# Output projection by seven products of sums: the last product accumulates in PSUM, the last stage runs in program order, weight sums are stored later, two small reorderings

## The chip, the cores and the metric

The kernel runs on 1 core of one Trainium2 chip (trn2). The metric is the device time of one execution in microseconds, from the first to the last work of the core. Three executions are given for the kernel before; one further execution was profiled.

## What is computed

One layer of a hybrid backbone, D_MODEL 1024, 1024 latent tokens and 256 context tokens. Cut to what matters here:

```python
mod = jax.nn.silu(c) @ w_ada + b_ada
shift, scale, gate = jnp.split(mod, 3, axis=-1)
hl = rmsnorm(x, norm_g) * (1.0 + scale) + shift
zl = jnp.split(hl @ w_in, PROJ_SPLITS, axis=-1)
ya = short_conv_branch(zl[0], zl[1], zl[2], zl[3], conv_sc)
yb = neighbourhood_attention(heads(zl[4]), heads(zl[5]), heads(zl[6]), kc, vc, rpb) * jax.nn.silu(zl[7])
yc = conformer_branch(zl[8], zl[9], zl[10], conv_cf, conv_cf_b, ln_cf_g, ln_cf_b)
y = jnp.concatenate([ya, yb, yc], axis=-1) @ w_out
x = x + gate * y
return rmsnorm(x, final_g)
```

All inputs are fp32. `kc` and `vc` come from the context tokens through the same weights. The conformer branch has a depthwise convolution of 31 taps and a layer norm.

## The kernel before, in words

**Precision.** Every matmul operand is split into two fp32r parts (`split`, L127): ScalarE copies the high part, VectorE or GpSimd subtracts it to get the low part. A product is three matmuls: high by high, high by low, low by high.

**Stages.** (1) `start` (L978): loads, the adaLN matmuls and the normalised, transposed input, in an order written out by hand in the string `SEQ` (L51). A letter is an operation, a digit its block: `B` are the adaLN matmuls of a block, `R` the copy of their result by ScalarE, `C` its four transposes and the shift and scale made of them by VectorE, `f` and `u` the modulation (ScalarE) and the split (VectorE) of a block of the input, `m` the six matmuls that use it, `D` matmuls on zeros that keep TensorE active. (2) The input projections, with four head pairs of attention between them. In each step of `attention` (L531) a block of scores (L596, L597) goes to PSUM, VectorE adds the bias and takes the minimum (L601), ScalarE takes the exponential (L604), GpSimd normalises (L606), TensorE transposes (L615), the result is split (L619, L620) and multiplied by the values (L627). Keys are split into `kt` by `sink_k` (L368). Weights of the projections are loaded into `wr` by SP (L310) and split into `wh` and `wl` by ScalarE and GpSimd (L129, L130). (3) The output projection, at the end of `build`.

**Background work.** `spawn` and `poll` (L95, L105) interleave generators with the matmuls: a generator yields the microseconds of planned matmul time after which its next piece is issued. Two of them are touched here. `out_weights` (L852) makes four sums of quarters of `w_out` in eight blocks (GpSimd subtracts, the result is split, SP stores it to DRAM as `T1` to `T4`, L874). `cf_norm` (L703) transposes the convolution's result in two groups for each half, normalises it on VectorE with a reciprocal root from GpSimd (L271), and transposes it back (L734).

**Order of the engines.** TensorE runs in program order. On VectorE (DVE), ScalarE (ACT), GpSimd (POOL) and SP a scheduler sets the order, except in `start`.

**The output projection.** `y` (1024 by 1024) and `w_out` are taken as 2 by 2 quarters A and B and multiplied by seven products of sums (Winograd's form of Strassen's scheme) instead of eight. One product of a half by a half is 48 matmuls of 512 columns: four row tiles by four blocks of the inner dimension by three parts. The products in order: A11 B11 and A12 B21 (their sum is C11, rows 0 to 3 in half `h0`), S2 T2 (added to A11 B11, called `u` or U2), S1 T1 (with U2 it makes `v`, which belongs to C12 and C22), S3 T3, S4 B22 (to C12: rows 0 to 3, half `h1`), A22 T4 (to C21: rows 4 to 7, half `h0`). C22 is rows 4 to 7, half `h1`. `out_mm4` (L915) issues a product with the inner blocks outside and the four row tiles inside, so all four finish within its last twelve matmuls.

**After the products.** `out_part` (L927): VectorE multiplies a result in PSUM by the gate (L933), adds it to the residual `xres` (L934), and ScalarE sums the squares (L941). `out_gain` (L943) multiplies by `final_g` on GpSimd (L945), `out_mean` (L947) turns the first sum of squares into a mean (L951). When both halves of a row tile are there, `out_scale` (L956) makes the reciprocal root on GpSimd (L961, L964), ScalarE scales the half that has its gain (L967), VectorE scales the other one (L971), and SP stores both (L975). Of row tile 7 the last product comes in two halves of 256 columns.

GpSimd's eight instructions on `u` (four tiles by two), L1263 to L1270:

```python
for t in range(4):
    V.tensor_tensor(out=u[t], in0=ps[t], in1=u[t], op=ALU.add)
    self.out_part(t + 4, h1, 0, ps[t], lp, S)
    self.out_mean(t + 4, 0)
    G.tensor_tensor(out=u[t], in0=u[t], in1=self.gate[:, h0], op=ALU.mult)
    x = self.xres[t + 4][0][:, h0]
    G.tensor_tensor(out=x, in0=x, in1=u[t], op=ALU.add)
    self.out_gain(t + 4, h1)
```

## Time and profile before

| | |
|---|---|
| median of 3 executions | 626.82 us (626.68 to 627.6) |
| the profiled execution | 627.2 us, of which the span of the instructions is 625.2 us |
| TensorE (PE) busy | 582.7 us, 93% of the span, 3041 matmuls |
| VectorE (DVE) busy | 439.3 us, 70% |
| ScalarE (ACT) busy | 264.6 us, 42% |
| GpSimd (POOL) busy | 241.8 us, 39% |
| chain that ended last, by engine | PE 58%, DVE 12%, SP's queue 9%, DMA 6%, POOL 6%, ACT 4%, issue 4% |
| DMA | 98.56 MB, mean 158 GB/s |

How to read it: a busy share is an average over all stages, and matmuls overlap, so a duration of one is longer than the distance to the next. The chain that ended last is followed back from the last instruction to whatever released it. "Idle before" is the time an engine stood still ahead of an instruction, with what ended it. The granted clock (PEclk) is a share of TensorE's full clock: 1.00 is 2.4 GHz, 0.50 is 1.2 GHz. Times in the rows are microseconds from the start of the span.

### The profile page before, as it was taken

The page shows a single profiled execution, that of the slowest core. Times are in us where ns is not written, and L with a number is a line of the kernel's source. Part 1 is how long each engine was busy: PE and PEld are TensorE (multiplying, and loading weights), DVE is VectorE, ACT ScalarE, POOL GpSimd, SP SyncE. Part 2 cuts the span into 40 slices and gives each one's busy share as a digit, 9 for nine tenths or more (in the row PEclk, how much of TensorE's full clock was granted, in tenths as well). Part 3 has the DMA queues.
Part 4 walks back from the last instruction along what each step waited for, and adds up shares of the span by engine and source line. Part 5 has one row for each costly group of instructions (what it writes and reads, how often), then busy time and mean ns, then how long its engine had stood idle before and what let it go on. Part 6 is the DMA issues. An engine that isn't in the chain of part 4 may idle for free.

```text
span 625.2 us, 9212 instructions
## 1 busy us (share of the span) xinstructions
PE 582.7 (93%) x3041; PEld 485.7 (78%) x3041; DVE 439.3 (70%) x744; ACT 264.6 (42%) x528; POOL 241.8 (39%) x270
## 2 busy tenths in 40 slices
PE   7799999999997999999999999999999999999950
PEld 5466888888896988798877898888887888788840
DVE  4466989666774699478897666936889446879935
ACT  2455721111444542556523656435554342443223
POOL 1031232001546334555444455345433440055863
PEclk9999999999998999899999999999999999999995
DMA  8991595966435348435257362483310663992224
GB/s 283 357 326 47 186 285 151 117 156 181 125 90 162 87 128 224 111 93 130 70 160 185 78 183 79 120 241 91 98 26 18 216 222 120 383 369 69 69 93 175
DMA packets 114434, 98.56 MB, mean 158 GB/s; under 512 B 27771, under 2 KB 94421, under 8 KB 114389
## 3 DMA queue, kind: packets, MB, share of 16 engines
q1 hardware_dynamic: 112517, 91.44, 50.6%
q10 hardware_dynamic: 1872, 6.55, 2.8%
q8 instruction: 24, 0.39, 0.3%
q14 instruction: 21, 0.17, 0.1%
HBM read 67.46 MB, written 22.68 MB: 144 GB/s over the span
## 4 chain that ended last, share of the span: by engine, by line
PE 58%; DVE 12%; SPq 9%; DMA 6%; POOL 6%; ACT 4%; issue 4%; DVEq 0%; ACTq 0%; POOLq 0%
PE ps_z L329 9%; PE ps_z L331 9%; PE ps_z L330 9%; SPq L509 4%; PE ps_t L615 3%; PE po L627 3%; DMA wr<-in_w_in 3%; DVE acc L692 3%; PE ps_z L419 3%; PE ps_z L421 3%; PE ps_z L420 3%; PE ps_s L596 3%; PE ps_s L597 2%; SPq L364 2%; DMA yc<-gd 1%
## 5 line engine op out<-in xcount | busy, mean ns | idle before, releaser
L329 PE MATMUL ps_z<-h,wh 128*128 128x512 f32 x384 | 152.3, 397 | 0.0
L331 PE MATMUL ps_z<-h,wl 128*128 128x512 f32 x384 | 151.2, 394 | 0.0
L330 PE MATMUL ps_z<-h,wh 128*128 128x512 f32 x384 | 150.7, 393 | 0.0
L130 POOL TENSOR_TENSOR wl<-wr,wh 128x512 fp32r<-128x512 f32 x44 | 60.1, 1370 | 142.8 <-ACT wh L129 136.2
L606 POOL TENSOR_SCALAR pr<-pr,sm 128x640 f32<-128x640 f32 (+1 forms) x64 | 55.7, 871 | 99.8 <-DVE sm L605 88.4
L331 PEld LDWEIGHTS ps_z<-h,wl 128*128 128x128 f32 x384 | 72.6, 189 | 16.3
L692 DVE SCALAR_TENSOR_TENSOR acc<-t,half_w,acc 128x1024 f32<-128x1024 f32 x60 | 82.2, 1369 | 1.2
L330 PEld LDWEIGHTS ps_z<-h,wh 128*128 128x128 f32 x384 | 73.0, 190 | 12.7
L329 PEld LDWEIGHTS ps_z<-h,wh 128*128 128x128 f32 x384 | 73.0, 190 | 12.3
L619 ACT ACTIVATE pw<-ps_t 128x640 fp32r<-128x640 f32 (+1 forms) x64 | 43.4, 679 | 74.2 <-PE ps_t L615 74.1
L601 DVE CUSTOM_DVE_ANT_0 ps_s<-ps_s,bt 128x640 f32<-128x640 f32 (+1 forms) x64 | 50.9, 796 | 26.3 <-PE ps_s L597 24.4
L620 DVE TENSOR_TENSOR pw<-ps_t,pw 128x640 fp32r<-128x640 f32 (+1 forms) x64 | 50.4, 788 | 22.2 <-ACT pw L619 21.8
L604 ACT ACTIVATE pr<-ps_s,mn 128x640 f32<-128x640 f32 (+1 forms) x64 | 49.0, 766 | 18.8 <-DVE mn L601 17.9
L627 PE MATMUL po<-pw,vt 128*128 128x256 f32 x304 | 51.9, 299 | 0.2 <-DVE pw L620 0.2
L129 ACT ACTIVATE wh<-wr 128x512 fp32r<-128x512 f32 x46 | 28.9, 629 | 54.3 <-DMA wr<-in_w_in 34.8
L596 PE MATMUL ps_s<-kt,qd 128*128 128x384 f32 (+1 forms) x128 | 40.5, 338 | 4.9 <-ACT pr L604 4.8
L615 PE MATMUL ps_t<-ident,pr 128*128 128x128 f32 x304 | 43.7, 273 | 0.8 <-DVE sm L605 0.6
L627 PEld LDWEIGHTS po<-pw,vt 128*128 128x128 f32 x304 | 40.5, 190 | 1.0 <-DVE pw L620 0.9
L597 PE MATMUL ps_s<-kt,qd 128*128 128x256 f32 x128 | 35.7, 284 | 3.0 <-DVE kt L380 3.0
L615 PEld LDWEIGHTS ps_t<-ident,pr 128*128 128x128 f32 x304 | 35.3, 141 | 3.2 <-issue 2.2
L130 POOL TENSOR_TENSOR bgp<-bg,bgp 128x256 fp32r<-128x256 f32 x32 | 28.0, 874 | 19.2 <-ACT bgp L129 19.2
L596 PEld LDWEIGHTS ps_s<-kt,qd 128*128 128x128 f32 x128 | 24.1, 188 | 11.9 <-ACT pr L604 9.9
(192 smaller groups left out, 1084.9 us busy)
## 6 DMA issues: line engine op xcount, KB each, us to landing
wr<-in_w_in SPq DMA_DIRECT2D x52, 256.0 KB
wa<-in_w_ada SPq DMA_DIRECT2D x16, 512.0 KB
qd<-qn SPq DMA_DIRECT2D x32, 256.0 KB
wT<-bgp SPq DMA_DIRECT2D x32, 256.0 KB
wt<-wT SPq DMA_DIRECT2D x16, 512.0 KB
vd<-t SPq DMA_DIRECT2D x20, 256.0 KB
x_in<-in_x SPq DMA_DIRECT2D x8, 512.0 KB
t<-in_w_ada SPq DMA_DIRECT2D x16, 256.0 KB
```

Source lines behind the costliest of these rows:

```text
L130: i2 = (eng or nc.vector).tensor_tensor(out=lo, in0=src, in1=f32(hi), op=ALU.subtract)
L329: nc.tensor.matmul(ps, lhsT=wh, rhs=hh, start=(k == 0), stop=False)
L330: nc.tensor.matmul(ps, lhsT=wh, rhs=hl, start=False, stop=False)
L331: self.last = nc.tensor.matmul(ps, lhsT=wl, rhs=hh, start=False, stop=(k == KT - 1))
L596: nc.tensor.matmul(win, lhsT=q[:, b % 4], rhs=kwin, start=(i == 0), stop=(i == 1))
L601: nc.vector.tensor_tensor_reduce(s, s, tb, op0=ALU.add, op1=ALU.min, scale=1.0, scalar=3e38, accum_out=mn)
L604: nc.scalar.activation(out=pr, in_=s, func=AF.Exp, scale=-1.0, bias=mn, accum_out=sm)
L606: nc.gpsimd.tensor_scalar(out=pr, in0=pr, scalar1=sm, scalar2=0.5, op0=ALU.mult, op1=ALU.mult)
L615: nc.tensor.transpose(out=pt[:, c * P:(c + 1) * P], in_=pr[:, c * P:(c + 1) * P], identity=self.ident)
L620: nc.vector.tensor_tensor(out=pw[:, :, 1, :], in0=pv, in1=f32(pw[:, :, 0, :]), op=ALU.subtract)
L627: self.nc.tensor.matmul(po, lhsT=vt[:, vi, h], rhs=pw[:, c], start=(c == 0), stop=(c == n - 1))
L692: self.after_pe(nc.vector.scalar_tensor_tensor(out=acc, in0=u[:, t:t + T], scalar=self.half_w[:, 2 * t + ct:2 * t + ct + 1], in1=acc, op0= ...
```

## The change

Five things are changed. In the output projection the last product, A22 T4, is accumulated in PSUM onto S3 T3, so that their sum is read once; T4 is stored with its sign turned, and U2 times the gate is added to the residual by GpSimd right after S2 T2. The tiles of the last two products are issued with the row tiles outside, and each row tile's scaling stands behind the next tile's addition. From S2 T2 on DVE, ACT, POOL and SP run in program order; the gate's row broadcast (`gate_rows`) moves behind A12 B21, the loads of `xres` 4 to 7 ahead of the split of S3. The weight sums are stored two steps after they are split, with longer gaps between blocks and a step of 2.9 instead of 3.2. `SEQ` has two matmuls on zeros ahead of `C1` and `m1` behind it. `cf_norm` waits 5.5 instead of 3.0 ahead of the transposes back, and 2.0 instead of 3.0 between its groups.

```diff
@@ -52,7 +52,7 @@
 X0 X1 X2 X3 L00 K L01 W00 W10 L10 L11 X4 X5 X6 X7 W01 W11 L20 L21 L30 L31 X8 X9
 q00 q11 r02 q20 x0 x1 q31 r22 x2 x3 D29 B00 D02 B01 a0 w001 R0 a1 w101 C0 a22 D07
 f0 f1 a3 u0 u1 m0 B10
-B11 R1 m1 C1 D03 q40 f2 f3 q51 u2 u3 m2 D03 r42 q60 q70 x4 x5 r62 x60 x7 m3 D02
+B11 R1 D02 C1 q40 f2 f3 m1 q51 u2 u3 m2 D02 r42 q60 q70 x4 x5 r62 x60 x7 m3 D02
 b0 b1 g0 v0 g1 v1 w01 w11 B20 n0 b2 B21 n1 R2 b3 g2 v2 g3 v3 n2 C2 a4 n3 f4 u4 a5 f5 u5
 b4 B30 m4 g4 v4 b5 B31 g5 v5 R3 m5 C3 n4 a6 f6 u6 a7 f7 u7 q80 n5 b6 g6 v6 q90 m6 b7 g7 v7 r82 m7 x8 n6 x9
 O Q00 c0 c1 h0 o0 h1 o1 Q01 n7 c2 c3 h2 o2 h3 o3 Q02 Q10 Q11 Q12
@@ -726,7 +726,7 @@
                                             op0=ALU.subtract, op1=ALU.mult)
                 vts.append(vt)
                 self.pe(0.43)
-                yield 3.0
+                yield (2.0, 5.5)[g]
             for ct in range(2):
                 ps = self.ps_z.tile([P, HALF], F32, name="ps_z", tag="z")
                 for j in range(4):
@@ -853,6 +853,11 @@
 
         nc = self.nc
         n = 256
+        kept = []
+
+        def put(name, p, i, c):
+            nc.sync.dma_start(out=self.wtd[name][:, :, i, c:c + n], in_=f32(p))
+
         for i in range(4):
             for c in range(0, HALF, n):
                 def raw(k, half):
@@ -862,16 +867,19 @@
 
                 b11, b12, b21, b22 = raw(i, 0), raw(i, 1), raw(4 + i, 0), raw(4 + i, 1)
                 t1 = pool.tile([P, n], F32, name="bg", bufs=5)
-                yield gap
-                for name, out, x, y in (("T1", t1, b12, b11), ("T3", b12, b22, b12), ("T2", t1, b22, t1), ("T4", t1, t1, b21)):
+                yield 2 * gap
+                for name, out, x, y in (("T1", t1, b12, b11), ("T3", b12, b22, b12), ("T2", t1, b22, t1), ("T4", t1, b21, t1)):
                     self.after_pe(nc.gpsimd.tensor_tensor(out=out, in0=x, in1=y, op=ALU.subtract))
                     yield gap
+                    if kept:
+                        put(*kept.pop())
                     p = pool.tile([P, 2, n], F32R, name="bgp", bufs=2)
-                    i1, i2 = self.split(p[:, 0], p[:, 1], out, nc.gpsimd)
-                    self.after_pe(i1)
-                    self.after_pe(i2)
+                    for ins in self.split(p[:, 0], p[:, 1], out, nc.gpsimd):
+                        self.after_pe(ins)
+                    kept.append((name, p, i, c))
                     yield gap
-                    nc.sync.dma_start(out=self.wtd[name][:, :, i, c:c + n], in_=f32(p))
+                yield gap
+        put(*kept.pop())
 
     def load_wt(self, name, pool):
         w = [pool.tile([P, 2, HALF], F32R, name="wt", bufs=8) for _ in range(4)]
@@ -930,7 +938,11 @@
         xt, ss = self.xres[tt]
         n = cs.stop - cs.start
         g = lp.tile([P, HALF], F32, name="fg", bufs=2)[:, 0:n]
-        nc.vector.tensor_tensor(out=g, in0=ps[:, 0:n], in1=self.gate[:, cs], op=ALU.mult)
+        ps = ps if isinstance(ps, list) else [ps[:, 0:n]]
+        m = n // len(ps)
+        for i, p in enumerate(ps):
+            c = cs.start + i * m
+            nc.vector.tensor_tensor(out=g[:, i * m:(i + 1) * m], in0=p, in1=self.gate[:, c:c + m], op=ALU.mult)
         nc.vector.tensor_tensor(out=xt[:, cs], in0=xt[:, cs], in1=g, op=op)
         if eng is nc.vector:
 
@@ -1150,7 +1162,7 @@
         stv.close()
         self.qp = r(self.pool("qp", 2, side="right"))
         self.pp = r(self.pool("pp", 2, side="right"))
-        self.spawn(self.out_weights(r(self.pool("bg", 1, side="right")), 3.2), 4.0)
+        self.spawn(self.out_weights(r(self.pool("bg", 1, side="right")), 2.9), 4.0)
         self.q_first = self.q_parts(0, 0)
         fill = itertools.chain(self.cf_in(1), *(f(ct) for ct in range(2) for f in (self.sc_in, self.sc_mid, self.sc_out)))
         self.run(self.proj_gate(0))
@@ -1214,7 +1226,6 @@
                 S.activation(out=u[t], in_=ps[t], func=AF.Copy)
             for tt in range(4):
                 self.out_tile(tt, lp)
-            self.gate_rows(ps_g)
 
             s1 = []
             for i in range(4):
@@ -1228,6 +1239,7 @@
             t2 = self.load_wt("T2", wt)
             s2 = self.y_parts(yc, [y[i][:, h0] for i in range(4)])
             self.out_mm4(ps, a12, b21, False, skip=True)
+            self.gate_rows(ps_g)
             t1 = self.load_wt("T1", wt)
             s1 = self.y_parts(yc, s1)
             raw = [self.load_b(yc, 1, 1, q, name="yc") for q in (0, 2)]
@@ -1235,58 +1247,67 @@
                 self.out_part(t, h0, 0, ps[t], lp, S)
                 self.out_mean(t, 0)
                 self.out_gain(t, h0)
+            E = mybir.EngineType
+            es.enter_context(tc.manual_schedule(engines={E.DVE, E.Activation, E.Pool, E.SP}))
             ps = banks(g=True)
             self.out_mm4(ps, s2, t2)
             t3 = self.load_wt("T3", wt)
-            s3 = self.y_parts(yc, [y[i][:, h1] for i in range(4)])
+            for tt in range(4, 8):
+                self.out_tile(tt, lp)
             for t in range(4):
                 V.tensor_tensor(out=u[t], in0=ps[t], in1=u[t], op=ALU.add)
-            for tt in range(4, 8):
-                self.out_tile(tt, lp)
+                v = lp.tile([P, HALF], F32, name="fw", bufs=2)
+                x = self.xres[t + 4][0][:, h0]
+                G.tensor_tensor(out=v, in0=u[t], in1=self.gate[:, h0], op=ALU.mult)
+                G.tensor_tensor(out=x, in0=x, in1=v, op=ALU.add)
+            s3 = self.y_parts(yc, [y[i][:, h1] for i in range(4)])
             ps = banks()
             self.out_mm4(ps, s1, t1)
+            s4 = self.y_parts(yc, [y[4 + i][:, h0] for i in range(4)])
             b22 = self.load_wt("B22", wt)
             for q in (0, 2):
                 self.split_b(b22, raw[q // 2], q)
-            s4 = self.y_parts(yc, [y[4 + i][:, h0] for i in range(4)])
             for t in range(4):
-                v = lp.tile([P, HALF], F32, name="fv", bufs=2)
-                V.tensor_tensor(out=v, in0=ps[t], in1=u[t], op=ALU.add)
+                v = u[t]
+                V.tensor_tensor(out=v, in0=ps[t], in1=v, op=ALU.add)
                 V.tensor_tensor(out=v, in0=v, in1=self.gate[:, h1], op=ALU.mult)
                 for tt, eng in ((t + 4, V), (t, G)):
                     x = self.xres[tt][0][:, h1]
                     eng.tensor_tensor(out=x, in0=x, in1=v, op=ALU.add)
-            ps = banks(g=True)
-            self.out_mm4(ps, s3, t3)
+
+            q = [slice(c, c + 256) for c in (0, 256)]
+            ps7 = banks(g=True)
+            ps7q = [ps7[3][:, 0:256], banks(1)[0][:, 0:256]]
+            for i in range(4):
+                for t in range(3):
+                    self.out_mm(ps7[t], i, t, s3, t3, i == 0, i == 3, skip=True)
+                for j in range(2):
+                    self.out_mm(ps7q[j], i, 3, s3, t3, i == 0, i == 3, q[j].start, q[j].stop, skip=True)
             t4 = self.load_wt("T4", wt)
             a22 = self.y_parts(yc, [y[4 + i][:, h1] for i in range(4)])
             for t in range(4):
-                V.tensor_tensor(out=u[t], in0=ps[t], in1=u[t], op=ALU.add)
-                self.out_part(t + 4, h1, 0, ps[t], lp, S)
+                self.out_part(t + 4, h1, 0, ps7[t] if t < 3 else ps7q, lp, S)
                 self.out_mean(t + 4, 0)
-                G.tensor_tensor(out=u[t], in0=u[t], in1=self.gate[:, h0], op=ALU.mult)
-                x = self.xres[t + 4][0][:, h0]
-                G.tensor_tensor(out=x, in0=x, in1=u[t], op=ALU.add)
                 self.out_gain(t + 4, h1)
-            ps = banks()
-            self.out_mm4(ps, s4, b22)
-            for t in range(4):
-                self.out_part(t, h1, 1, ps[t], lp, S)
-                self.out_scale(t, 1, ((h0, S, sync), (h1, None, sync)))
-            ps = banks(3, True)
-            for t in range(3):
+            ps = banks(3)
+            ps = ps + ps[0:1] + ps7
+            for t in range(7):
                 for i in range(4):
-                    self.out_mm(ps[t], i, t, a22, t4, i == 0, i == 3)
-                self.out_part(t + 4, h0, 1, ps[t], lp, S, ALU.subtract)
-                self.out_scale(t + 4, 1, ((h1, S, sync), (h0, None, sync)))
-
-            ps = banks(2)
-            q = [slice(c, c + 256) for c in (0, 256)]
+                    if t < 4:
+                        self.out_mm(ps[t], i, t, s4, b22, i == 0, i == 3)
+                    else:
+                        self.out_mm(ps[t], i, t - 4, a22, t4, False, i == 3, skip=True)
+                cs = h1 if t < 4 else h0
+                self.out_part(t, cs, 1, ps[t], lp, S)
+                if t:
+                    self.out_scale(t - 1, 1, last)
+                last = (h0 if t < 4 else h1, S, sync), (cs, None, sync)
             for j in range(2):
                 for i in range(4):
-                    self.out_mm(ps[j], i, 3, a22, t4, i == 0, i == 3, 256 * j, 256 * j + 256)
-                self.out_part(7, q[j], 1 + j, ps[j], lp, (S, V)[j], ALU.subtract)
+                    self.out_mm(ps7q[j], i, 3, a22, t4, False, i == 3, q[j].start, q[j].stop, skip=True)
+                self.out_part(7, q[j], 1 + j, ps7q[j], lp, (S, V)[j])
                 if j == 0:
+                    self.out_scale(6, 1, last)
                     self.out_gain(7, q[0])
                     self.out_mean(7, 1)
             self.out_scale(7, 2, ((h1, S, act), (q[0], V, None), (q[1], None, sync)))
```

**TensorE, in the first stage, after the adaLN matmuls of block 1 (L220).** `ps_a` is that block's PSUM tile, `ada_row` its copy, `ps_z` with `h` are the matmuls of an input block. Before:

```order
L220 MATMUL ps_a<-wa,stat 32x512 x8
L1066 MATMUL ps_z<-h_82,wh 128x512
...
L1069 MATMUL ps_z<-h_83,wh 128x512 x2
L232 MATMUL ps_a<-ident,ada_row 128x128 x4
L1036 MATMUL ps_z<-zero,ones_r 128x512 x3
```

Now:

```order
L220 MATMUL ps_a<-wa,stat 32x512 x8
L1048 MATMUL ps_z<-zero,ones_r 128x512 x2
L232 MATMUL ps_a<-ident,ada_row 128x128 x4
L1078 MATMUL ps_z<-h_82,wh 128x512
...
L1081 MATMUL ps_z<-h_83,wh 128x512 x2
```

The four transposes of `ada_row` stand ahead of the six matmuls of `m1`, behind two matmuls on zeros.

**SP's queue, at the start of head pair 1.** `qd` are queries, `wr` weights of the gate's projection, `wT` stores of weight sums, `bg` loads for them. Before:

```order
L364 DMA qd<-qn 64x2x512 x2
L874 DMA wT_69<-bgp 256x1x256
L364 DMA qd<-qn 64x2x512
L874 DMA wT_71<-bgp 256x1x256
L364 DMA qd<-qn 64x2x512
L860 DMA bg<-in_w_out 128x256 x3
L310 DMA wr<-in_w_in 128x4x128 x2
L874 DMA wT_70<-bgp 256x1x256
```

Now:

```order
L364 DMA qd<-qn 64x2x512 x4
L310 DMA wr<-in_w_in 128x4x128 x2
L859 DMA wT_69<-bgp 256x1x256
L865 DMA bg<-in_w_out 128x256
L310 DMA wr<-in_w_in 128x4x128 x2
```

Two stores and three loads for the weight sums no longer stand ahead of the first two weight loads.

**GpSimd, in the output projection.** `fu` (and `fw`) is U2 or v, `wt` the split of B22, `fv` the v of before. Before:

```order
L130 TENSOR_TENSOR wt<-yc,wt 128x512 x3
L1258 TENSOR_TENSOR xres<-xres,fv 128x512
L130 TENSOR_TENSOR wt<-yc,wt 128x512
L1258 TENSOR_TENSOR xres<-xres,fv 128x512 x3
L1267 TENSOR_TENSOR fu_5591<-fu_5591,gate 128x512
L1269 TENSOR_TENSOR xres<-xres,fu_5591 128x512
...
L1267 TENSOR_TENSOR fu_5597<-fu_5597,gate 128x512
L1269 TENSOR_TENSOR xres<-xres,fu_5597 128x512
...
L945 TENSOR_TENSOR xres<-xres,fgam 128x512
L961 TENSOR_SCALAR fss<-fss 128x1
```

Now:

```order
L1261 TENSOR_TENSOR fw<-fu_5589,gate 128x512
L1262 TENSOR_TENSOR xres<-xres,fw 128x512
...
L1261 TENSOR_TENSOR fw<-fu_5595,gate 128x512
L1262 TENSOR_TENSOR xres<-xres,fw 128x512
L130 TENSOR_TENSOR wt<-yc,wt 128x512 x4
L1276 TENSOR_TENSOR xres<-xres,fu_5589 128x512
...
L957 TENSOR_TENSOR xres<-xres,fgam 128x512
L973 TENSOR_SCALAR fss<-fss 128x1
```

The eight instructions on U2 stand ahead of the split of B22 and of v, and no longer among the gains ahead of the first reciprocal root.

## Rows read from the trace of the kernel before

**Rows 1.** Busy time by stretch: length, then PE, PEld, DVE, ACT, POOL, PEclk, DMA.

```profile
580.00:591.00 11.00, 11.00 (x49) 9.03 (x49) 10.95 (x17) 2.90 (x8) 8.85 (x8) 1.00 0.22 73
591.00:602.30 11.30, 11.28 (x61) 9.55 (x60) 2.48 (x3) 1.45 (x4) 10.57 (x12) 1.00 0.00 0
602.30:625.20 22.90, 0.00 (x0) 0.00 (x0) 13.83 (x24) 9.90 (x20) 7.73 (x16) 0.60 0.49 183
```

**Rows 2.** The chain that ended last, from 600 us on: start, us, what.

```profile
601.61 0.27 POOL fss L961
...
603.77 0.75 DVE xres L971
604.52 0.61 DVE xres L934
...
606.98 0.75 DVE xres L971
...
620.41 0.35 DVE xres L969
```

**Rows 3.** GpSimd's busy time from its first gain to the first reciprocal root.

```profile
549.60:601.60 52.00, 37.53 (x32) 1.00 0.38 134
```

**Rows 4.** Groups by line: shapes, count, busy us, mean ns of one, idle before.

```profile
L1269 POOL TENSOR_TENSOR xres<-xres,fu 128x512 f32<-128x512 f32 x4 | 6.3, 1568 | 0.3
L1267 POOL TENSOR_TENSOR fu<-fu,gate 128x512 f32<-128x512 f32 x4 | 6.2, 1546 | 1.8 <-DVE fu L1264 1.8
L1258 DVE TENSOR_TENSOR xres<-xres,fv 128x512 f32<-128x512 f32 x4 | 6.0, 1498 | 0.0
L130 POOL TENSOR_TENSOR wt<-yc,wt 128x512 fp32r<-128x512 f32 x4 | 5.6, 1409 | 6.8 <-ACT wt L129 5.3 <-issue 1.4
L1258 POOL TENSOR_TENSOR xres<-xres,fv 128x512 f32<-128x512 f32 x4 | 5.6, 1394 | 4.3 <-DVE fv L1255 4.3
```

**Rows 5.** VectorE in order of time.

```profile
556.23 2.07 DVE L1243 TENSOR_TENSOR fu<-ps_g,fu 128x512 f32<-128x512 f32 x3 [1.39 <-PE ps_g L913]
...
567.22 0.69 DVE L1254 TENSOR_TENSOR fv<-ps_f,fu 128x512 f32<-128x512 f32 x1
...
581.26 0.68 DVE L1264 TENSOR_TENSOR fu<-ps_g,fu 128x512 f32<-128x512 f32 x1
...
589.19 1.38 DVE L933 TENSOR_TENSOR fg<-ps_f,gate 128x512 f32<-128x512 f32 x2
...
602.54 0.78 DVE L971 SCALAR_TENSOR_TENSOR xres<-xres,fss,fgam 128x512 f32<-128x512 f32 x1 [9.07 <-POOL fss L964]
```

**Rows 6.** What TensorE waited for: us in total, times, longest.

```profile
PE ps_s L596 <- ACT pr L604: 4.8, 5, 3.0
PE ps_s L597 <- DVE kt L380: 3.0, 2, 1.9
...
PE ps_z L734 <- DVE t L724: 1.6, 2, 1.1
...
PE ps_g L843 <- DMA yc<-gd: 0.5, 1, 0.5
```

**Rows 7.** Busy time by stretch behind 252 us, columns as in Rows 1.

```profile
252.00:254.00 2.00, 2.00 (x7) 1.61 (x7) 1.15 (x3) 0.78 (x2) 1.88 (x2) 0.50 0.36 89
254.00:256.00 2.00, 2.00 (x9) 1.64 (x8) 0.16 (x1) 0.00 (x0) 0.69 (x1) 0.72 0.74 204
```

**Rows 8.** SP's queue and ScalarE in order of time, start of head pair 1.

```profile
246.13 0.98 SPq L310 DMA_DIRECT2D wr<-in_w_in  x2
...
249.98 0.63 ACT L129 ACTIVATE wh<-wr 128x512 fp32r<-128x512 f32 x1 [1.97 <-DMA wr<-in_w_in]
```

**Rows 9.** ScalarE and TensorE in order of time, first stage.

```profile
26.52 0.60 ACT L225 ACTIVATE ada_row<-ps_a 128x512 f32<-128x512 f32 x1 [3.42 <-PE ps_a L220]
...
27.87 0.60 PE L232 MATMUL ps_a<-ident,ada_row 128*128 128x128 f32 x4
...
30.70 0.50 PE L1066 MATMUL ps_z<-h,wh 128*128 128x512 f32 x1 [1.54 <-DVE h L300]
```

## The prediction

> **What bounds the kernel now.** I read the stretches first. TensorE is busy until 602.3 us, all but without a gap in the output projection, and then 22.9 us pass in which it does nothing [rows 1]: the kernel has a TensorE-bound body and a tail. The chain that ended last says who owns the tail. It runs over GpSimd's reciprocal roots, VectorE's scaling and addition and ScalarE's squares, one row tile after the other: from the scaling at 603.77 to the next at 606.98 it is 3.21 us for one tile, and its first piece is the reciprocal root at 601.61 [rows 2]. What the reader is to see next is why that root came so late. VectorE had stood still for 9.07 us for it, from 593.5 on, with PSUM results waiting [rows 5]. GpSimd was not short of time: from 549.6 to 601.6 it was busy 37.5 of 52.0 us [rows 3], 14.5 us idle. But eight of its instructions (U2 times the gate, added to the residual) could start only behind VectorE's addition of S3 T3 to u at 581.26 [rows 5], and they take 6.2 + 6.3 = 12.5 us [rows 4]. So the root waits for work that could not begin earlier, not for too much work. In the body I read TensorE's waits [rows 6] and the clock behind them [rows 7].
>
> My sum is made against the profiled execution: 627.2 us with a span of 625.2, so 2.0 us lie around the span. The median is 0.4 us below that execution. About 0.2% (1.3 us) is what a measurement here can tell from no change.
>
> **The end, part by part.** *GpSimd.* The eight instructions move behind S2 T2, whose sums VectorE makes from 556.23 on, the first by 556.9 [rows 5]. The gains of tiles 0 to 3 stand ahead of them in GpSimd's order; I leave 0.6 us for that, so the eight run from 557.5 to 570. The four low parts of B22 follow (5.6 us, to 575.6) and the four additions of v (5.6 us, to 581.2) [rows 4]. S4 B22 starts at 580 [rows 1], so B22 is ready by 4 us; that is the cover, and if it goes, TensorE waits at the start of S4 B22. At 581 GpSimd then owes only four means and gains of C22, which come when VectorE delivers.
>
> *VectorE.* Four additions to u of 0.68 us go, 2.4 us at a distance of 0.60. But the sixteen instructions on v and the splits took from 567.22 to 581.26 today [rows 5], and the splits of S3 and S4 ahead of them now meet GpSimd's moved work. An addition with both inputs in SBUF took 1.50 us there, while GpSimd was at work, against 0.69 for one that reads PSUM [rows 4, 5]. I take 2 us of delay from that and begin C22 at 583.2. C22's four tiles took 589.19 - 581.26 = 7.9 us [rows 5]; without the additions to u they take 5.5, and with the halves of tile 3 and GpSimd's gains 6.2. So VectorE reaches tile 0 of the last stage at 589.4, as today: it gains nothing by itself.
>
> *The first root.* Tile 7's gain on GpSimd ends near 592, the root of tile 0 at 592.9, so VectorE scales tile 0 at 593.0 instead of 602.54: **9.6 us earlier**.
>
> *From there to the end.* The scaling of tile t-1 now stands behind the addition of tile t, so the squares and the root of a tile run beside VectorE's work on the next. A tile costs VectorE two instructions of 0.61 us and one of 0.75 [rows 2], 2.0 us, instead of 3.2. Scaling tile 0 (0.7), tiles 2 to 6 with the scalings behind them (10.0) and the first half of tile 7 (1.0) reach 604.7; the root of tile 6 comes at 604.9; its scaling, the second half, its squares, mean and root add 3.3 (608.2). From the last scaling's first row to the end of the span it is 625.2 - 620.41 = 4.8 us [rows 2]. That is 613.0. Small terms: `gate_rows` no longer waits for its load, -0.5 [rows 6]; twelve more half-width matmuls cost at most the 0.3 us by which the last stretch, which has 24 of them, exceeds 11.0 [rows 1], and are hidden since VectorE ends last. Row tile 3 of S4 B22 takes tile 0's bank, free at 589.4 + 0.7 = 590.1, and would start at 580 + 36 x 11.0/48 = 588.2 [rows 1]: TensorE waits 1.9 us and ends at 604, which VectorE (at 606) doesn't notice. The span would end at **612.9 instead of 625.2: -12.3**. Bounds: if GpSimd never held VectorE, the same sum is 610.7; if each of the eight two-SBUF additions of C22 and of tiles 0 to 3 cost 1.50 us instead of 0.61, it is 7 us more, 620. I take the first value that the mixed rows give, since after 592 GpSimd has only roots left.
>
> The Trainium skill ("SBUF — State Buffer", section "SBUF: two separate sides") says that a VectorE instruction with two SBUF inputs and a GpSimd instruction lock one port pair for a whole instruction. By that rule the sum is 612.9, without it 610.7; the trace's 1.50 against 0.69 us agrees with the rule, so it lowers the chance of the second rival below.
>
> **The body.** *First stage.* The transposes of C1 start at 27.87, behind six matmuls, and the chain from them ends in a wait of 1.54 us at 30.70 [rows 9]. Now two matmuls on zeros stand there, and the copy of the adaLN rows by ScalarE ends at 26.52 + 0.60 [rows 9], so they start at 27.2, 0.65 us earlier and all behind them follows: -0.65 (0 to -1.5, the whole wait).
>
> *Head pair 1.* Weights issued by SP at 246.13, behind three loads and two stores for the weight sums, reach ScalarE at 249.98 after 1.97 us of waiting [rows 8], which holds the split of the keys and so TensorE for 1.9 us [rows 6]. Behind that wait the clock is 0.50 for a stretch of 2 us and 0.72 for the next [rows 7], 1.2 GHz instead of 2.4: another 1.6 us lost. The loads now go first, some 3 us earlier: -3.3, bounds 0 and -3.6.
>
> *Longer waits ahead of L734.* Its two waits, 1.6 us together [rows 6], are shorter than the 2.5 us added: -1.6 (bounds 0 and -1.6).
>
> *What stays.* The longest wait, 3.0 us for the exponential [rows 6], has the same weight loads ahead of it in SP's queue; one cast more now stands ahead of ScalarE's work there. I take 0.5 for new waits of this kind (bounds: -4.6, that wait and its clock gone, and +4.6, one more such). The stores two steps late take no time of their own; their blocks are 11 steps of 2.9 instead of 9 of 3.2 us, so the last of the eight comes 8 x (31.9 - 28.8) = 25 us of planned time later, inside head pair 3 and still ahead of the loads of T2.
>
> Body: -0.65 - 3.3 - 1.6 + 0.5 = -5.0. Span: 625.2 - 12.3 - 5.0 = 607.9; with 2.0 around it 609.9, and 0.4 less for the median: **609.5 us**.
>
> **The rivals.** *First: only the end gains.* The scheduler moves all of ScalarE's and SP's work in the heads, so a wait may appear for each that goes. For it: the 3.0 us wait stays. Against it: the weight loads of pair 1 do stand earlier. Then 625.2 - 12.3 + 2.0 - 0.4 = 614.5.
>
> *Second: VectorE keeps pace with TensorE.* If GpSimd doesn't hold it, the additions follow the matmuls tile by tile, and the end is 2.2 us earlier: 607.3, down to 604.5 if part of the 3.0 us wait goes as well. Against it: the 1.50 us rows.
>
> *Third: the end stays late.* The moved work delays B22's split beyond 580 and the C22 gains with it, so the first root comes at about 601 as today; only the 2.7 us of the shorter tile cycle and the 5.0 of the body remain: 619. For it: GpSimd's 24 wide instructions before the root stay 24. Against it: the 14.5 us of idle time.
>
> *Fourth, slower: the clock.* The place is a head's second half, where ScalarE's cast of new weights stands ahead of its exponential. If weights land over 2 us after the cast's turn, TensorE waits and its clock halves, 3.0 + 1.6 = 4.6 us each time by today's longest. It decides from four such new waits on (18.4 against the 17.3 gained), which gives 628.3. For it: the reordered queue; against it: one wait of that length in the whole trace today.
>
> **How the numbers follow.** Forecast 0.62 (its own range 606.5 to 612.5), first rival 0.18, second 0.13, third 0.05, fourth 0.02. The range reaches from the second rival's lower end, 604.5, to 616, past the first rival, and leaves out about 0.1. Slower by over 0.2% is the fourth alone, 0.02; within 0.2% takes a mix of the third and fourth, 0.01; faster 0.97.
>
> **What would show it.** Right: the first reciprocal root of the last stage near 593 minus the body's gain, VectorE's 9 us wait gone, a distance of about 2 us between the scalings, the tail behind the last matmul 8 to 10 us; in the body no wait at L597 of pair 1 and no half clock behind it, none at L734. Wrong: GpSimd still at wide work when the last stage's squares are done, or TensorE waiting for a PSUM bank or for B22 by more than 2 us, or new waits for the exponential with half clock behind them.

## The result, and the profile after

The changed kernel takes **616.88 us** in the median of 4 executions (616.56 to 618.25); the kernel before takes 626.75 us in the executions beside them (626.45 to 627.6). The ratio is **0.9845**, 95% interval 0.9826 to 0.9863: faster by 1.5%. The forecast was 609.5 us, its range 604.5 to 616.0: the direction is right, the gain is 9.9 instead of 17.3 us, and the time lies 0.9 us above the range. The span of the profiled execution is 615.3 us, 625.2 before.

The first view to read is VectorE in order of time at the end (start, us, instruction, in brackets the idle time ahead of it), the answer to [rows 5].

```profile
551.92 2.75 DVE L1258 TENSOR_TENSOR fu<-ps_g,fu 128x512 f32<-128x512 f32 x4 [2.73 <-PE ps_g L921]
554.59 12.85 DVE L130 TENSOR_TENSOR yc<-y,yc 128x512 fp32r<-128x512 f32 x8
567.36 0.68 DVE L1272 TENSOR_TENSOR fu<-ps_f,fu 128x512 f32<-128x512 f32 x1
568.07 1.04 DVE L1273 TENSOR_TENSOR fu<-fu,gate 128x512 f32<-128x512 f32 x1
569.14 1.67 DVE L1276 TENSOR_TENSOR xres<-xres,fu 128x512 f32<-128x512 f32 x1
...
580.00 3.60 DVE L130 TENSOR_TENSOR yc<-y,yc 128x512 fp32r<-128x512 f32 x4
583.51 0.68 DVE L945 TENSOR_TENSOR fg<-ps_g,gate 128x512 f32<-128x512 f32 x1
...
590.06 0.68 DVE L945 TENSOR_TENSOR fg<-ps_f,gate 128x512 f32<-128x512 f32 x1
590.84 1.25 DVE L946 TENSOR_TENSOR xres<-xres,fg 128x512 f32<-128x512 f32 x1
...
594.86 0.75 DVE L983 SCALAR_TENSOR_TENSOR xres<-xres,fss,fgam 128x512 f32<-128x512 f32 x1 [0.80 <-POOL fss L976]
...
596.85 0.74 DVE L983 SCALAR_TENSOR_TENSOR xres<-xres,fss,fgam 128x512 f32<-128x512 f32 x1
```

Three things are to be seen. VectorE's wait of 9.07 us for the first root is now 0.80. From 551.92 to that wait VectorE has no idle time at all: it is the bound of this stretch. And it is slow: the eight splits of S3 and S4 take 12.85 us, 1.6 each, while an addition that reads PSUM takes 0.68. Of `v`, the one that reads PSUM (L1272) keeps its 0.68, the two with both inputs in SBUF take 1.04 and 1.67.

GpSimd's groups by line (shapes, count, busy us, mean ns of one) answer to [rows 4], where the same work took 1.41, 1.55 and 1.57 us:

```profile
L130 POOL TENSOR_TENSOR wt<-yc,wt 128x512 fp32r<-128x512 f32 x4 | 6.8, 1736 | 0.0
L1261 POOL TENSOR_TENSOR fw<-fu,gate 128x512 f32<-128x512 f32 x4 | 6.6, 1642 | 0.0
L1262 POOL TENSOR_TENSOR xres<-xres,fw 128x512 f32<-128x512 f32 x4 | 6.5, 1625 | 0.3
```

What TensorE waited for (us in total, times, longest), the answer to [rows 6]:

```profile
PE ps_s L596 <- ACT pr L604: 7.8, 9, 4.1
PE ps_f L919 <- DVE fg L945: 5.6, 1, 5.6
...
PE ps_s L597 <- DVE kt L380: 2.0, 2, 1.0
```

The waits at L734 (1.6 us) and for the gate's load (0.5) are gone, as is the wait of 1.9 us at L597 of pair 1; the waits for the exponential grew from 4.8 to 7.8. New is one wait of 5.6 us that ends at 590.8 us: row tile 3 of S4 B22 takes tile 0's bank, which VectorE reads only at 590.06. Behind it the clock falls. Busy time by stretch, columns as in [rows 1]:

```profile
590.80:593.00 2.20, 2.20 (x5) 1.81 (x6) 2.06 (x3) 0.87 (x4) 2.04 (x3) 0.50 0.00 0
593.00:595.00 2.00, 2.00 (x6) 1.52 (x5) 1.20 (x2) 0.85 (x3) 1.75 (x4) 0.50 0.00 0
595.00:596.30 1.30, 1.30 (x5) 0.99 (x5) 1.26 (x3) 0.58 (x1) 1.22 (x2) 0.61 0.00 0
596.30:598.00 1.70, 1.70 (x9) 1.40 (x8) 1.70 (x3) 0.97 (x3) 0.23 (x2) 1.00 0.83 308
```

So two suspects stand for the missing gain of the end: VectorE held by GpSimd's moved work, or the wait of TensorE with its half clock.

### The profile page after: what moved, and what is told of

It is laid out like the page before. It is cut to its first block, busy times and chain, and to the rows that moved or that the text cites. A ratio compares the mean times of both kernels' runs of the same rounds, so it can differ in the third digit from the quotient of the medians.

```text
span 615.3 us, 9220 instructions
## 1 busy us (share of the span) xinstructions
PE 582.6 (95%) x3051; PEld 486.5 (79%) x3051; DVE 440.4 (72%) x741; ACT 264.0 (43%) x528; POOL 246.3 (40%) x270
## 4 chain that ended last, share of the span: by engine, by line
PE 62%; DVE 12%; DMA 6%; SPq 6%; ACT 5%; issue 4%; POOL 3%; DVEq 0%; POOLq 0%; ACTq 0%
PE ps_z L329 10%; PE ps_z L331 10%; PE ps_z L330 10%; PE po L627 4%; PE ps_t L615 4%; DMA wr<-in_w_in 4%; PE ps_z L419 3%; PE ps_z L421 3%; PE ps_z L420 3%; PE ps_s L596 3%; DVE yc L130 3%; PE ps_s L597 2%; SPq L509 2%; ACT pr L604 2%; PE ps_f L919 2%
## 5 line engine op out<-in xcount | busy, mean ns | idle before, releaser
L130 POOL TENSOR_TENSOR wl<-wr,wh 128x512 fp32r<-128x512 f32 x44 | 61.2, 1394 | 133.8 <-ACT wh L129 130.5
L330 PEld LDWEIGHTS ps_z<-h,wh 128*128 128x128 f32 x384 | 72.1, 188 | 12.3
L329 PEld LDWEIGHTS ps_z<-h,wh 128*128 128x128 f32 x384 | 72.3, 188 | 12.0
L596 PE MATMUL ps_s<-kt,qd 128*128 128x384 f32 (+1 forms) x128 | 40.7, 339 | 7.8 <-ACT pr L604 7.8
L597 PE MATMUL ps_s<-kt,qd 128*128 128x256 f32 x128 | 35.7, 284 | 2.0 <-DVE kt L380 2.0
L596 PEld LDWEIGHTS ps_s<-kt,qd 128*128 128x128 f32 x128 | 24.2, 189 | 15.5 <-ACT pr L604 13.2
```

Of the source, the lines that this page charges most:

```text
L130: i2 = (eng or nc.vector).tensor_tensor(out=lo, in0=src, in1=f32(hi), op=ALU.subtract)
L329: nc.tensor.matmul(ps, lhsT=wh, rhs=hh, start=(k == 0), stop=False)
L330: nc.tensor.matmul(ps, lhsT=wh, rhs=hl, start=False, stop=False)
L596: nc.tensor.matmul(win, lhsT=q[:, b % 4], rhs=kwin, start=(i == 0), stop=(i == 1))
```

## The experiments

For every kernel the profile gives three marks: the first sum of S2 T2 on VectorE (what comes before it is the body), the distance from it to the first scaling in the last stage, and the distance from it to the end of the span. The ratio is to the kernel before on the same chip.

| kernel | sum of S2 T2 at | to first scaling | to the end | median us | ratio and interval |
|---|---|---|---|---|---|
| before | 556.2 | 46.3 | 69.0 | 626.75 | 1 |
| changed | 551.9 | 42.9 | 63.4 | 616.88 | 0.9845 (0.9826 to 0.9863) |
| after2 | 551.5 | 42.9 | 63.8 | 617.88 | 0.9879 (0.9860 to 0.9899) |
| e_front | 550.8 | 46.3 | 69.0 | 623.77 | 0.9966 (0.9945 to 0.9987) |
| e_end | 559.4 | 42.9 | 63.5 | 621.05 | 0.9933 (0.9909 to 0.9957) |
| e_no_u2 | 552.6 | 37.1 | 56.4 | 611.05 | 0.9759 (0.9727 to 0.9791) |
| e_late | 553.1 | 37.1 | 59.1 | 614.65 | 0.9819 (0.9778 to 0.9859) |
| e_half_order | 555.7 | 40.2 | 61.2 | 617.27 | 0.9867 (0.9847 to 0.9887) |
| e_order | 555.3 | 43.0 | 62.4 | 618.19 | 0.9884 (0.9867 to 0.9902) |
| e_bank | 554.8 | 43.0 | 63.8 | 617.96 | 0.9881 (0.9844 to 0.9918) |
| e_slack | 553.1 | 38.0 | 58.8 | 614.69 | 0.9809 (0.9779 to 0.9840) |
| e_slack_lag | 551.7 | 38.5 | 57.7 | 612.48 | 0.9774 (0.9744 to 0.9803) |
| p_ow | 557.1 | 46.3 | 69.0 | 625.05 | 0.9978 (0.9957 to 0.9999) |
| p_cf | 554.3 | 46.3 | 69.0 | 624.72 | 0.9968 (0.9947 to 0.9989) |

The end repeats to some tenths wherever its code is the same (46.3 to the first scaling in each kernel with the old end, 42.9 to 43.0 with the new). The body does not: with the same code it ended between 550.8 and 555.7. So what an edit of the end does is read from the distances, and the medians say whether it can be measured.

### The two halves of the change: e_front, e_end, after2

`e_front` is the kernel before with the first hunks of the change (the sign of T4 as before); `e_end` is the changed kernel without them; `after2` is the changed kernel again.

```diff
+B11 R1 D02 C1 q40 f2 f3 m1 q51 u2 u3 m2 D02 r42 q60 q70 x4 x5 r62 x60 x7 m3 D02
...
+                yield (2.0, 5.5)[g]
...
+                    if kept:
+                        put(*kept.pop())
...
+        self.spawn(self.out_weights(r(self.pool("bg", 1, side="right")), 2.9), 4.0)
```

> The kernel before with the three changes ahead of the output projection alone (the order of the first stage, the waits of cf_norm, the weight sums stored two steps behind); its end stays. If the body gave what the two traces show at the sums of S2 T2 (4.3 us earlier, of which 0.5 belong to gate_rows): 626.75 - 3.8 = 622.9. If my forecast for the body holds, 621.8. If the end was what moved the body's events (ScalarE and SP have other work ahead of it there), under 2 us of gain, over 624.8.

> The kernel before with the changed end alone (the first stage's order, cf_norm's waits and the stores of the weight sums as before; the sign of T4 turned as the end needs it). In the two profiles the end is shorter by 69.0 - 63.4 = 5.6 us from the sums of S2 T2 on. If the end's gain is that, 626.75 - 5.6 = 621.1, a gain of 0.9%. If my forecast for the end holds (12.3 us), 614.4. If the order written out for the engines also moved work of the body, another start of S2 T2's sums than 556.2.

> The changed kernel once more, unaltered, beside the others of this call: 616.9 if its body's waits come out as in the first profile (S2 T2's sums at 551.9); the kernels with the same body had them between 551.9 and 554.8, so 616.5 to 619.

Measured: the body alone gains 0.34%, 2.1 us (0.8 to 3.4), where 3.8 was expected from the two traces; the end alone 0.67%, 4.2 us (2.7 to 5.7); both together, timed beside `e_end`, 1.21%, 7.6 us (6.3 to 8.8). The parts add up to 6.3, the lower edge of the whole's interval. The end's distance is 63.4 to 63.8 us with either body, 5.2 to 5.6 shorter than before, so the 12.3 us forecast for it are refuted, and nothing in the body took the end's gain away.

### GpSimd's moved work left out: e_no_u2

```diff
-                v = lp.tile([P, HALF], F32, name="fw", bufs=2)
-                x = self.xres[t + 4][0][:, h0]
-                G.tensor_tensor(out=v, in0=u[t], in1=self.gate[:, h0], op=ALU.mult)
-                G.tensor_tensor(out=x, in0=x, in1=v, op=ALU.add)
```

> The changed kernel without GpSimd's eight instructions of 128x512 that add U2 times the gate to the residual of rows 512 to 1023, columns 0 to 511 (so that part of the output lacks U2). If GpSimd and VectorE hold each other there, VectorE's eight splits of S3 and S4 fall from 1.6 to about 0.7 us each and end near 561, v begins when S1 T1 is there (about 563 instead of 567.4), the last stage begins 4.4 us earlier, the wait for tile 0's bank falls from 5.6 to about 1.3 us and its half clock goes: about 611. If the time is set by the shared bank or by the written-out order of the engines and GpSimd's work is hidden, it stays at 616.9, within 1 us.

Measured: 611.05 us. VectorE in order of time:

```profile
552.56 2.75 DVE L1258 TENSOR_TENSOR fu<-ps_g,fu 128x512 f32<-128x512 f32 x4 [2.74 <-PE ps_g L921]
555.23 4.29 DVE L130 TENSOR_TENSOR yc<-y,yc 128x512 fp32r<-128x512 f32 x7
560.77 0.69 DVE L130 TENSOR_TENSOR yc<-y,yc 128x512 fp32r<-128x512 f32 x1 [1.25 <-ACT yc L129]
563.54 0.69 DVE L1268 TENSOR_TENSOR fu<-ps_f,fu 128x512 f32<-128x512 f32 x1 [2.08 <-PE ps_f L921]
...
574.71 3.60 DVE L130 TENSOR_TENSOR yc<-y,yc 128x512 fp32r<-128x512 f32 x4
578.22 0.68 DVE L945 TENSOR_TENSOR fg<-ps_g,gate 128x512 f32<-128x512 f32 x1
...
589.65 0.75 DVE L983 SCALAR_TENSOR_TENSOR xres<-xres,fss,fgam 128x512 f32<-128x512 f32 x1 [0.81 <-ACT fsq L953]
```

The splits of S3 and S4 take 0.61 us from one to the next instead of 1.6, VectorE waits 1.25 and 2.08 us where it had no idle time, and `v` begins 11.0 us behind the sums of S2 T2 instead of 15.4. The first scaling comes 5.8 us earlier, TensorE's wait for the bank is 0.8 us, and the clock stays. The expectation from the hold, about 611, was met; that GpSimd's work is hidden is refuted. It is mutual: without the eight, B22's low parts take 1300 ns each.

```profile
L130 POOL TENSOR_TENSOR wt<-yc,wt 128x512 fp32r<-128x512 f32 x4 | 5.1, 1300 | 8.3 <-ACT wt L129 7.1 <-issue 1.2
```

The Trainium skill ("SBUF — State Buffer", section "SBUF: two separate sides") calls the port pair that GpSimd shares with VectorE's instructions on two SBUF inputs an exclusive lock, held for a whole instruction. The trace agrees in kind: 1.6 against 0.69 us on VectorE, 1.74 against 1.30 on GpSimd, and 0.68 to 0.69 in both kernels for the addition that reads PSUM. In size it shows somewhat less: strictly one behind the other, a VectorE split (0.61 us) and a GpSimd instruction (1.30) would take 1.91 us, and such a pair took 1.6 to 1.7.

### The same sum made elsewhere: e_late, e_half_order

`e_late` gives VectorE one more addition for each of the row tiles 4 to 7 in the last stage, from PSUM, and GpSimd none. `e_half_order` leaves GpSimd tiles 6 and 7, gives VectorE 4 and 5, and has the order of tiles of `e_order` below.

```diff
+            if u is not None:
+                nc.vector.tensor_tensor(out=gp, in0=p, in1=u, op=ALU.add)
+                p = gp
```

> The changed kernel with U2 added by VectorE in the last stage (one more addition from PSUM of about 0.69 us for each of the row tiles 4 to 7) in place of GpSimd's eight instructions; the output is complete. If GpSimd and VectorE hold each other, it has the gain of the kernel without U2 less 4 x 0.69 = 2.8 us: about 613.5. If GpSimd's work is hidden, the four additions are added to the end: 619.5.

> A version meant to beat both: GpSimd adds U2 to row tiles 6 and 7 alone (four instructions, in a stretch where VectorE waited 3.3 us for TensorE in the kernel without U2), VectorE adds it to tiles 4 and 5 in the last stage, and the order of the tiles is that of the run before; complete output. If the hold is mutual and only its part behind VectorE's slack counts, it is the kernel without U2 plus 2 x 0.69 us: about 612.5, 4.4 less than the changed kernel. If each of the four still delays v, about 614.7.

`e_late` came out between the two expected times, nearer to that of the hold: its first scaling is that of `e_no_u2` (37.1), its end 2.7 us later, as four additions of 0.68 cost. `e_half_order` missed its 612.5 us: in the median it is no faster than the changed kernel timed beside it (617.27 against 617.88). By the distance to the end it gains 2.2 to 2.6 us, as the second case of its expectation had it (each of the four still delays `v`); its body came out late (555.7). VectorE in order of time:

```profile
555.67 2.75 DVE L1262 TENSOR_TENSOR fu<-ps_g,fu 128x512 f32<-128x512 f32 x4 [2.74 <-PE ps_g L921]
558.34 13.31 DVE L130 TENSOR_TENSOR yc<-y,yc 128x512 fp32r<-128x512 f32 x8
571.58 0.68 DVE L1278 TENSOR_TENSOR fw<-ps_f,fu 128x512 f32<-128x512 f32 x1
...
595.89 0.75 DVE L987 SCALAR_TENSOR_TENSOR xres<-xres,fss,fgam 128x512 f32<-128x512 f32 x1 [0.81 <-ACT fsq L957]
```

GpSimd, with four instructions less, begins B22's low parts at 564.46, 8.8 us behind the sums instead of 14.9, and now these hold the second half of the splits. All eight splits again met a wide instruction of GpSimd, one each. VectorE's 3.3 us of waiting could not be used, since every split is drawn out while GpSimd has anything wide to do. By these two kernels the number of GpSimd's wide instructions counts: eight cost 42.9 - 37.1 = 5.8 us up to the first scaling, four cost 40.2 - 37.1 = 3.1, so **0.73 to 0.78 us each**.

### TensorE's wait: e_order, e_bank

```diff
-            for t in range(7):
+            tiles = (0, 1, 2, 4, 5, 3, 6)
+            for k, t in enumerate(tiles):
```

```diff
-            ps7q = [ps7[3][:, 0:256], banks(1)[0][:, 0:256]]
+            ps7q = [ps7[3][:, c] for c in q]
...
-            ps = banks(3)
-            ps = ps + ps[0:1] + ps7
+            ps = banks() + ps7
```

> The changed kernel with the last stage's row tiles in another order (0, 1, 2, 4, 5, 3, 6, 7): the tile that shares tile 0's bank comes two tiles later, when VectorE has long read tile 0. If TensorE's wait of 5.6 us is only a consequence of VectorE's lateness, the wait and the half clock go, the first scaling stays 42.9 us behind the sums of S2 T2, and only VectorE's 0.84 us of waiting for TensorE and the stretched cycles come back: 2.1 us less than the changed kernel. If the bank sets the time, 5.6 us less or more.

> The changed kernel with a PSUM bank of its own for row tile 3 of S4 B22 (tile 3 of S3 T3 stays whole in one bank, its two halves are two column ranges of it). If VectorE's lateness is what counts and the waiting TensorE is its consequence, the wait of 5.6 us and the half clock go, but the first scaling stays near 594.9, and only the 0.8 us that VectorE later waits for TensorE and the stretched tile cycles come back: about 2 us, 614.9. If the shared bank is the cause, the whole wait comes back: about 611. If the halves now wait for each other in one bank, up to 1 us is lost at the end: 617.9.

In `e_order` the wait at the bank is 0.2 us:

```profile
PE ps_f L919 <- DVE fg L945: 0.2, 1, 0.2
```

The first scaling stays 43.0 us behind the sums, and the end comes 1.0 us nearer than in the changed kernel (62.4 against 63.4, and 1.4 nearer than in `after2`), where 2.1 was expected; the median shows nothing of it (618.19 against 617.88 for `after2`). So TensorE's 5.6 us and its half clock are a consequence, worth 1.0 to 1.4 us. `e_bank` says the same of the first scaling, but made a worse wait at the end. In it the sums of row tile 7's two halves are begun in one bank, and its output is not whole; it is read for the waits alone.

```profile
PE ps_g L919 <- DVE fg L945: 9.6, 1, 9.6
```

The last product's matmuls for the second half of tile 7 do not begin before VectorE has read the first half in that bank, and VectorE then waits 1.37 us for them. What the bank of its own gave, this wait took back.

### Beating both: e_slack, e_slack_lag

`e_slack` is `e_late` with the sums of tiles 6 and 7 made by VectorE between the splits of S3 and S4, where it waited. `e_slack_lag` moreover lets the scaling of a tile stand behind the addition of the tile after the next.

```diff
+            for t in (2, 3):
+                v = lp.tile([P, HALF], F32, name="fw", bufs=2)
+                x = self.xres[t + 4][0][:, h0]
+                V.tensor_tensor(out=v, in0=u[t], in1=self.gate[:, h0], op=ALU.mult)
+                V.tensor_tensor(out=x, in0=x, in1=v, op=ALU.add)
...
+                todo.append((t, 1, ((h0 if t < 4 else h1, S, sync), (cs, None, sync))))
+                if t > 1:
+                    self.out_scale(*todo.pop(0))
```

> A version meant to beat both, complete output: no U2 on GpSimd; VectorE adds U2 to row tiles 6 and 7 between the splits of S3 and S4 (four instructions, 2.8 us, where it waited 1.3 + 2.1 us for ScalarE and TensorE in the kernel without U2) and to tiles 4 and 5 in the last stage (2 x 0.69 us). If what counts is how many of GpSimd's wide instructions run beside VectorE's, the stretch from the sums of S2 T2 to the end is that without U2 plus 1.4: 57.8 us, against 63.4 in the changed kernel; about 612. If VectorE's own four instructions delay the sums v as GpSimd's did, 60.5, about 614.5.

> The same, and the scaling of a tile stands behind the addition of the tile after the next, until tile 6. If VectorE's 0.81 us of waiting for the first square and root is on the path, the end is 57.0 us behind the sums of S2 T2 (0.8 less than without this step); if the last tiles pay it back, 57.8.

`e_slack` ends 58.8 us behind the sums, 0.3 less than `e_late`, where 57.8 was expected: the splits of S4, now later, meet B22's low parts (4.70 us for four), and `v` begins 12.4 us behind the sums, 11.0 in `e_no_u2`. `e_slack_lag` took 1.1 us more off the end, where 0.8 was expected, and so reached 57.7 instead of 57.0: it has no wait ahead of the first scaling. VectorE in it:

```profile
551.72 2.75 DVE L1262 TENSOR_TENSOR fu<-ps_g,fu 128x512 f32<-128x512 f32 x4 [2.73 <-PE ps_g L921]
554.39 2.49 DVE L130 TENSOR_TENSOR yc<-y,yc 128x512 fp32r<-128x512 f32 x4
...
559.46 4.70 DVE L130 TENSOR_TENSOR yc<-y,yc 128x512 fp32r<-128x512 f32 x4
564.08 0.68 DVE L1277 TENSOR_TENSOR fw<-ps_f,fu 128x512 f32<-128x512 f32 x1
...
590.24 0.76 DVE L987 SCALAR_TENSOR_TENSOR xres<-xres,fss,fgam 128x512 f32<-128x512 f32 x1
```

It is the fastest complete kernel: 612.48 us, ratio 0.9774, and its interval (to 0.9803) lies wholly below that of `after2` (from 0.9860). From `e_late` and `e_slack` it is not told apart by the times alone: their intervals overlap its own.

### Parts of the body: p_ow, p_cf

Each is the kernel before with one hunk of those of `e_front`: the weight sums, or the waits of `cf_norm`.

> The kernel before with the weight sums' stores two steps behind alone. By my forecast the wait at pair 1 (1.9 us) and the half clock behind it (1.6 us) go and nothing else moves: 3.3 us less than before, 622.5. If the waits only move to the heads of pair 0, under 1 us of gain, over 624.8, with longer waits for the exponential near 160 and 194 us in its trace.

> The kernel before with cf_norm's two waits of 2.0 and 5.5 instead of 3.0 and 3.0 alone. By my forecast the two waits ahead of L734 go, 1.6 us less than before, 624.2. If other waits for the exponential take their place in pair 3, under 0.5 us of gain.

Measured: 1.4 us (0.1 to 2.7) and 2.0 us (0.7 to 3.3). The forecast's 3.3 us for the weight sums lies above the first interval; its 1.6 for `cf_norm` lies inside the second. What TensorE waited for in `p_ow`:

```profile
PE ps_s L596 <- ACT pr L604: 7.1, 6, 3.2
PE ps_s L597 <- DVE kt L380: 2.9, 2, 1.6
...
PE ps_z L734 <- DVE t L724: 1.0, 2, 0.7
```

and in `p_cf`, which has no wait at L734:

```profile
PE ps_s L596 <- ACT pr L604: 7.1, 10, 1.7
PE ps_s L597 <- DVE kt L380: 2.9, 2, 1.8
```

The wait at pair 1 (251 to 254 us) is gone in every kernel with the new weight sums and stands in `p_cf` (1.8 us) and `e_end` (2.0). In its place every one of the former has a wait of 0.3 to 1.9 us for the keys' split of pair 3 (421 to 426 us), which is in none of the latter. That the last blocks of the weight sums now stand ahead of pair 3's weights is the likely way; it was not tried by itself. The waits for the exponential near 162 us came out between 0.5 and 3.0 us in kernels with the same code; they scatter, and no edit here explains them.

## Why the prediction was right in its direction and wrong in its size

**What bounds the kernel: right.** The tail was a late root, not too much work. Once the eight instructions moved, the wait of 9.07 us fell to 0.80 and the last stage went at 2.0 us a tile (594.86, 596.85), as the sum had it.

**GpSimd: right in order, long in time.** The eight were to run from 1.3 to 13.8 us behind the sums of S2 T2; they ran from 1.7 to 15.0. B22's low parts were ready at 573.67, 3.1 us ahead of S4 B22 (576.78): of the 4 us of cover 3.1 were left, and that was enough.

**VectorE: the step that failed.** "I take 2 us of delay from that and begin C22 at 583.2" puts C22 27.0 us behind the sums of S2 T2; it began 31.6 us behind them. `e_no_u2` has 25.7, so the hold costs 5.9 us up to there and not 2, and C22 came 4.6 us later than the forecast. The mechanism was the one named, the term was mis-sized, and the rows had its size: eight splits stood beside eight wide instructions of GpSimd, and at 1.50 against 0.69 us [rows 4, 5] that is 8 x 0.81 = 6.5. The prediction made such a product only as a bound, and for other additions: the eight of C22 and of tiles 0 to 3. Another 1.5 us came after C22 had begun (11.3 instead of 9.8 us to the first scaling): four additions beside GpSimd's gains took 1.25 to 1.31 us, and the root came 0.80 late. Together 6.1 us: the first scaling is 42.9 us behind the sums, the forecast had 36.8. The 1.5 us are not the eight's: `e_no_u2` also needs 11.4 us there, and that its 37.1 lies so near the forecast's 36.8 is luck (25.7 + 11.4 against 27.0 + 9.8). Two of the prediction's own signs of being wrong were there: GpSimd at its gains when the first root was due, and TensorE waiting over 2 us for a bank.

**From the first scaling to the end: right.** The terms reach from 593.0 to 613.0, 20.0 us; 20.4 were measured. (The forecast's 612.9 does not come out of its own terms: 613.0 less the 0.5 for `gate_rows` is 612.5; the other 0.4 us stands in no term.) TensorE's wait for tile 0's bank was 5.6 instead of 1.9 us, with half clock, and VectorE did notice: it waited 0.17 and 0.67 us for TensorE, and `e_order` gets 1.0 us back.

**The body: the named waits went, the forecast gain was too large.** In the two profiled executions the sums of S2 T2 came 4.3 us earlier, of which 0.5 are `gate_rows`: 3.8 against 5.0 forecast. The timed gain is smaller, 2.1 us (0.8 to 3.4), and 3.8 and 5.0 both lie above it. The first stage gave 1.0 (the same matmuls of the input's transposes at 61.47 instead of 62.48), forecast 0.65; pair 1's wait of 1.9 with its 1.6 of half clock went (3.5, forecast 3.3), and so did L734's 1.6. These make 6.1, so the term that failed is the 0.5 us for new waits: by the remainder it was 2.3 (6.1 - 3.8) to 4.0 (6.1 - 2.1). In the trace the waits for the exponential grew by 3.0 us in all, and the wait at pair 3, 1.0, is new. The latter comes with the weight sums, as `p_ow` shows; which part of the scatter near 162 and 193 us belongs to the change stays open.

**The rivals.** The first (only the end gains) did not happen: both halves gain. The second (VectorE keeps pace) did not happen either, and even `e_no_u2`, where the eight do not hold VectorE, takes 611.05 us and not the 607.3 of that rival. The third had the right count against the change, 24 wide instructions before and after, by the wrong way: B22's split was in time, and VectorE paid. The fourth did not happen: the waits for the exponential grew by 3.0 us (7.8 against 4.8), far from the four new ones of 4.6 us that it needed. Nor does each long wait halve the clock, as that rival took it: see the last section.

## What to carry to other kernels

Idle time on GpSimd does not make moved work free. Here it cost VectorE's instructions that read PSUM nothing; beside those with two SBUF inputs count pairs, one drawn-out VectorE instruction for each wide GpSimd instruction (here 0.73 to 0.78 us each), wherever in the stretch they meet. Before moving, ask what VectorE itself would pay: one addition from PSUM (0.68 us) was cheaper than two GpSimd instructions. An edit in a stretch that has some 4 us of scatter ahead of it (550.8 to 555.7 here) is read from the distance between two events of the stretch, not from the total.

## What the runs showed of the hardware that was not expected

While GpSimd ran wide instructions back to back, VectorE's instructions on SBUF alone went at GpSimd's pace, one for one: 12.85 us for eight beside eight, and 13.31 for eight beside eight others, against 0.61 from one to the next when alone. Filling VectorE's idle time in such a stretch gave nothing.

The length of a TensorE wait alone does not tell whether the clock falls. Near 193 us TensorE waits for the exponential ahead of its scores (L596): in the kernel before for 2.98 us, until 192.25, in `e_front` for 2.96 us, until 193.12. Behind the first wait the granted clock fell to 0.50, the lower of its two levels (1.2 of 2.4 GHz):

```profile
194.00:196.00 2.00, 2.00 (x7) 1.61 (x7) 0.42 (x2) 0.89 (x2) 1.15 (x1) 0.50 0.51 158
```

Behind the second it stayed at 1.00:

```profile
194.00:196.00 2.00, 2.00 (x15) 1.78 (x14) 1.26 (x3) 0.55 (x1) 0.18 (x1) 1.00 0.63 177
```

In `p_cf`, behind a wait of only 1.8 us that ended at 251.18, it fell to 0.54:

```profile
251.50:253.50 2.00, 2.00 (x8) 1.61 (x7) 1.19 (x3) 0.72 (x3) 2.00 (x3) 0.54 0.24 64
```

What decides between them is not shown by these runs.
